# Planned margins behind transfers and GpSimd's mask, and the inverse's PSUM banks shared with value and z-gate projections

## Chip, cores and metric

The kernel runs on one core of a Trainium2 chip. The metric is the device time of one execution in microseconds, the median of the runs. One execution was also profiled; all durations and waits below come from that one.

## What is computed

The reference is a trunk of two layers over 2048 frames of width 1024, with a conditioning vector `c`. Layer 1 is a Griffin recurrent block, layer 2 a gated DeltaNet with 8 heads of 128:

```python
for i in range(DEPTH):                                   # DEPTH = 2
    cond = c_act @ ada_w[i] + ada_b[i]                   # shift, scale, gate
    h = rmsnorm(x, norm_g[i]) * (1.0 + scale) + shift
    if i % N_MIXERS == 0:
        out = rglru_block(h, ...)       # linear, conv4, RG-LRU scan, * silu(z), linear
    else:
        out = gated_deltanet_block(h, ...)
    x = x + gate * out
return rmsnorm(x, final_g)

# inside gated_deltanet_block, per head and chunk:
qkv = silu(causal_dwconv(proj[..., :o1], conv_w)); z = proj[..., o1:o2]
q = l2norm(q) * DK ** -0.5; k = l2norm(k)
t_mat = triangular_solve(a_mat + eye, eye)               # inverse of the chunk's matrix
v_new = u_c - w_c @ state
o_c = q_c @ state + attn_c @ v_new
state = state * e_c + k_c.T @ v_new                      # chunk after chunk
o = rmsnorm(o) * onorm_g * silu(z); out = o @ out_w
```

All of it is float32. Large products are made of three products of split operands (high x high, high x low, low x high).

## The kernel before

**Stages.** The frames are worked on in two units of 1024, each in two halves of 512 columns. Layer 1 comes first: its input projection (panels of 128 output columns, eight for the recurrent branch x and eight for its gate z), convolution, gates and scan, then its output projection. Layer 2 follows: for each unit and head the projections k, v, q and at some heads z (`KINDS`, `ZS`), then the heads' recurrences, and at the end the output projection with the final norm.

**One projection.** `job` (L667) takes a weight panel that `panels_thread` (L608) has loaded as `raw`, cast to `whi` on ScalarE (L640) and completed by `wlo` (GpSimd at L646 in the first unit, a reload in the second). It takes a PSUM bank, issues 24 matmuls of 128x512 (L664 in `products`), and hands the bank to a thread that empties it: `conv2_thread` (L984) for k, v and q, which copies it to `xe` on ScalarE (L726 in `extend`) and then convolves it on VectorE (L714), or `zgate_thread` (L1015) for z, which reads it on ScalarE (L1019) and again on VectorE (L1021).

**PSUM.** There are eight banks, two under each of four tags. In layer 2, `mm` holds all projections, `tp` transposes and the products k k and q k, `d` the recurrence's tiles, and `c` the tiles `px` and `pr` of the inverse (`levels_thread`, L1300 on) and `pab` of the decay. Buffers of one tag are used in turn, so a new tile waits until the last tile but one of its tag is given back.

**One head of layer 2.** `key_thread` (L1110) loads the decay rows `ec` by broadcast, masks them on GpSimd (L1119), takes the exponential on ScalarE (L1123), and forms the chunk's matrix `ac` (L1169), whose 32x32 blocks go to memory. `inverses_thread` inverts the blocks on VectorE (L1285 and L1288, 31 steps), `levels_thread` joins them with small matmuls. `norm_q_thread` (L1191) turns the query through memory and takes its squares on ScalarE (L1203, tile `junkq`). `value_thread` (L1227) turns the value through memory (`tokens_of`, L1213, into `vn`) and scales it on ScalarE (L1239). `recurrence_thread` runs the chunks one after the other: `pp` (L1405), `zt` on VectorE (L1414), `py` (L1422), `yt` on ScalarE (L1428), `pS` (L1434), and the state on VectorE (L1447). `outputs_thread` (L1474) scales the head's output by `ro` and writes it to memory.

**Activations of later units.** `turned_thread` (L514) with `turn_thread` (L497) and `scale_thread` (L442) normalizes blocks of 128 rows, transposes them through a memory tile `xt_d`, and reloads them as `xk`.

**What sets the order.** Every piece above is a generator. `Weave` (L66) is a planner: it holds a planned time when each engine, the queue of transfers and each buffer come free, always takes the thread that can start first (ties by a priority), and writes that thread's instructions. So the order of the planned starts is the order of the instructions in each engine's queue, and the engines then run their queues in order. All transfers go through the one queue of SyncE. A thread says with its `yield` what it uses:

```python
elif w[0] == "sp":
    self.free["sp"] = t + 0.48
    self.free["dma"] = max(t + 1.13, self.free["dma"]) + w[1] / 360e3
    th.t = self.free["dma"] + self.SEEN if len(w) < 3 or w[2] else t + 0.48
elif w[0] == "none":
    th.t = t + max(w[1], 0.0)
else:
    self.free[w[0]] = t + w[1]
    th.t = t + w[1] + (w[2] if len(w) > 2 else self.LAG[w[0]])
```

`yield "act", 0.95` means that ScalarE is taken for 0.95 us and that the thread goes on after that and a lag (0.2 us for GpSimd and TensorE, 0.3 us for the other two). A third number replaces the lag. `yield "none", x` lets the thread alone wait for x planned microseconds. None of these numbers is an instruction.

Of the kernel before, what the change touches and what calls it, by code (L numbers as in the profile page):

```python
# [30 lines left out]
TURN = 2  # L31
BLK = 2
KTN, QTN = 6, 5
EPS = 1e-6


# [102 lines left out]
def trunk_kernel(ctx, tc, x, c, ada_w, ada_b, ada_c, norm_c, final_g, w1, cw1, cb1, gate_w, gate_b, lam, ow1,  # L139
# [299 lines left out]
        w.set(ev("gates"))  # L439


    def scale_thread(xt, done):  # L442
        stok = yield slots["ss"]
        rtok = yield slots["rs"]
        ttok = yield slots["tt"]
        yield "act", 1.04
        junk = tile_([P, D], "tt", "sqj", BF16)
        ss = tile_([P, 1], "ss", "ss")
        act.activation(junk, xt, AF.Square, accum_out=ss)
        put("tt", ttok)  # L450
        yield "pool", 0.75
        rs = tile_([P, 1], "rs", "rs")
        rsqrt(rs, ss, 1.0 / D, 1)
        put("ss", stok)
        yield "dve", STT
        dve.tensor_scalar(xt, xt, rs, None, ALU.mult)
        put("rs", rtok)
        w.set(done)
# [36 lines left out]
            put(tag, tok)  # L495

    def turn_thread(key, t_d, xt, tok, ttok, b):  # L497
        yield from scale_thread(xt, ev("scaled", key, b))
        for d in range(2):
            htok = yield slots["hf"]  # L500
            yield "dve", EV
            tb = tile_([P, KT * 2, 32], "hf", "xb")
            dve.transpose(out=tb, in_=xt[:, d * TC:(d + 1) * TC].rearrange("p (a j) -> p a j", j=32))
            if d == 1:
                put("b4", tok)
            dst = t_d[4 * d:4 * d + 4, :, b * P:(b + 1) * P].rearrange("k (r i) (c j) -> c i (k r) j", i=32, j=32)
            for c_ in range(4):
                yield "sp", 64 * KB, c_ == 3
                sp.dma_start(out=dst[c_], in_=tb[32 * c_:32 * c_ + 32])
            put("hf", htok)  # L510
        put("turn", ttok)
        w.set(ev("turned", key, b))
# [95 lines left out]
    def panels_thread():  # L608
        yield ev("small")
        ahead = []  # L610
        for name, panels, _ in plans:
            for m, p in enumerate(panels):

                if m == 2 and name == ("in2", 0):
                    yield ev("owt", 1, 1)
                    yield ev("gates")
                if m == 0 and name == ("in1", 0):
                    for q in panels[0:2]:
                        ahead.append((yield from panel_load(name, q)))
                    w.set(ev("firstpanels"))  # L620
                if m in (2, len(panels) - 1) or m < 2 and name != ("in1", 0):
                    if name == ("in1", 0):
                        yield ev("adaissue", 3)
                    ahead.append((yield from panel_load(name, p)))
                htok = yield slots["whi"]
                ltok = yield slots["wlo"]
                if not ahead:
                    ahead.append((yield from panel_load(name, p)))
                raw, rtok = ahead.pop(0)
                lo = tile_([P, KT, P], "wlo", "wlo", F32R)  # L630
                if name[1] > 0:

                    kept = yield ev("kept", p)
                    yield "sp", 512 * KB, False
                    sp.dma_start(out=f(lo), in_=kept)
                    w.spawn(arrive_thread(ev("lo", name, p)), 0)
                yield ev("raw", name, p)
                yield "act", 0.95
                hi = tile_([P, KT, P], "whi", "whi", F32R)
                act.copy(hi, raw)  # L640
# [26 lines left out]
    def job(name, jobs, n):  # L667
# [6 lines left out]
        if layer == 2 and kind in "kq":  # L674
            rtok = yield slots[kind + "t"]

        bank = "d" if layer == 1 and kind == "z" else "mm"
        mtok = yield slots[bank]
        pt = ps.tile([P, TC], F32, tag=bank, name="mm")
        yield from products(pt, (hi, lo), h, (lambda k: ev("split", (name, i), k)), 0.2275 if layer == 1 else MM)  # L680
# [3 lines left out]
        if layer == 1:  # L684
            w.spawn((conv1_thread if kind == "x" else z1_thread)(u, m, i, pt, mtok, bank), 2, 0.2)
        elif kind == "z":
            w.spawn(zgate_thread(u, m, i, pt, mtok), 6, 0.2)
        else:
            w.spawn(conv2_thread(u, kind, m, i, pt, mtok, rtok), 5, 0.2)
        if all(j != i for _, j in jobs[n + 1:]):  # L690
            w.set(ev("free", name, i))
        w.set(ev("job", name, n))
# [23 lines left out]
    def extend(xe, pt, mtok, carry, key, g):  # L716

        if g == 0:
            yield "pool", 0.1
# [4 lines left out]
            pool.tensor_copy(out=xe[:, 0:4], in_=carry)  # L724
        yield "act", CP
        act.copy(xe[:, 4:4 + TC], pt)  # L726
        put("mm", mtok)
        yield "pool", 0.14, 0.0
        pool.tensor_copy(out=carry, in_=xe[:, TC:TC + 4])
        w.set(ev("carry", key, g))  # L730
# [250 lines left out]
        w.set(ev("l2"))  # L981


    def conv2_thread(u, kind, h, i, pt, mtok, rtok):  # L984
# [4 lines left out]
        yield from extend(xe, pt, mtok, carry2[:, idx, :], (kind, h), u * NTC + i)  # L989
        ftok = yield slots["xf"]  # L990
        yield "pool", 0.68
        xf = tile_([P, TC], "xf", "xf")
# [19 lines left out]
        put("tt", ttok)  # L1012
        w.set(ev(kind, u, h, i), (r, rtok))

    def zgate_thread(u, h, i, pt, mtok):  # L1015
# [5 lines left out]
        dve.scalar_tensor_tensor(tz, tz, 1.0, pt, ALU.add, ALU.mult)  # L1021
        put("mm", mtok)
# [87 lines left out]
    def key_thread(u, h, i):  # L1110
# [4 lines left out]
        yield "sp", 256 * KB  # L1115
        ec = tile_([P, TB, P], "ec", "ec")
        sp.dma_start(out=ec, in_=g_d[h:h + 1, i * TC:(i + 1) * TC].to_broadcast([P, TC]))
        yield "pool", 0.7
        pool.affine_select(out=ec, in_=ec, compare_op=ALU.is_ge, fill=-1e30, base=0, pattern=[[0, TB], [1, P]],  # L1119
                           channel_multiplier=-1)  # L1120
        for b in range(TB):
# [69 lines left out]
    def norm_q_thread(u, h, i):  # L1191
# [3 lines left out]
        yield "sp", 256 * KB  # L1195
        pq = tile_([P, TB, P], "hf", "pq")
        sp.dma_start(out=pq, in_=q_d.rearrange("b p d -> p b d"))
        stok = yield slots["ssq"]
        ss = tile_([P, TB], "ssq", "ssq")
        for b in range(TB):  # L1200
# [12 lines left out]
    def tokens_of(ap, name):  # L1213
# [7 lines left out]
        for r in range(4):  # L1221
            yield "sp", 64 * KB, r == 3
            sp.dma_start(out=dst[r], in_=tb[32 * r:32 * r + 32])  # L1223
        put("hf", htok)
        return t_d

    def value_thread(u, h, i):  # L1227
# [5 lines left out]
        yield "sp", 256 * KB  # L1233
        vn = tile_([P, TB, P], "vn", "vn")
        sp.dma_start(out=vn, in_=v_d.rearrange("b p d -> p b d"))
        nk, ntok = (yield ev("key", u, h, i))[-2:]
        for b in range(TB):
            yield "act", 0.255, 0.0
# [235 lines left out]
    def outputs_thread(u, h, i, oo, otok, so, sotok):  # L1474
# [1 line left out]
            yield ev("o", u, h, i * TB + b)  # L1476
        rq, qtok = yield ev("rq", u, h, i)
        rtok = yield slots["ro"]
        yield "pool", 1.4
        ro = tile_([P, TB], "ro", "ro")  # L1480
        rsqrt(ro, so, 1.0 / P, TB)
        pool.tensor_tensor(ro, ro, rq, ALU.mult)
# [16 lines left out]
        for g in range(4):  # L1499
            yield "sp", 128 * KB, g == 3  # L1500
            sp.dma_start(out=dst[g], in_=ob[32 * g:32 * g + 32])
        put("hf", htok)
        w.set(ev("od", u, h, i))

# [276 lines left out]
```

## Time and profile before

| what | value |
|---|---|
| median of 3 runs | 1968.5 us |
| the runs | 1966.23, 1968.5, 1977.2 us |
| the profiled execution | 1969.04 us |
| its span from first to last instruction | 1967.3 us |
| mean granted TensorE clock | 0.983 |
| TensorE busy | 1849.4 us (94%) |
| VectorE, ScalarE, GpSimd busy | 1469.3, 1050.9, 640.5 us |
| transfers | 322.77 MB |

PE is TensorE's matmuls, PEld its weight loads, DVE VectorE, ACT ScalarE, POOL GpSimd, SP SyncE, which issues the transfers. A row of waits reads "who <- what ended the wait: total us, times, longest us". A row of the timeline gives start and duration in us, engine, line, operation, written and read tiles, shapes and count, and in square brackets the idle time of the engine just before it with what ended it. The granted clock is a share of full speed; where it is 0.5 a matmul takes twice its time.

### The profile page before, as it was taken

To read this page: it belongs to the slowest core of one execution; us is meant where nothing else is said; L and a number is where in the kernel's file an instruction comes from. 1 tells how busy PE (TensorE), PEld (TensorE's weight loads), DVE (VectorE), ACT (ScalarE), POOL (GpSimd) and SP (SyncE) were. 2 spreads that over 40 slices of the span, in tenths; PEclk is the share of its full clock that TensorE was granted. 3 is DMA by queue.
4 is the path that set the end of the run, shared out by engine and by line. 5 is a ranking of instruction groups with operands and counts; after the bars stand their busy time and mean duration, and the time that the engine had idled before them with its cause. 6 is when DMAs were issued, how large, how long until landed. Compare 5 with 4: busy or idle time off the path is not lost.

```text
span 1967.3 us, 31401 instructions
## 1 busy us (share of the span) xinstructions
PE 1849.4 (94%) x10286; PEld 1501.0 (76%) x10286; DVE 1469.3 (75%) x3271; ACT 1050.9 (53%) x2585; POOL 640.5 (33%) x1116
## 2 busy tenths in 40 slices
PE   6999898999999999998889999998999999999998
PEld 3777677887777777786777777777888888878887
DVE  6898888887645577878787888667777778876653
ACT  3667577766121345564655666465566566654221
POOL 3354532223000235344434543232332334410101
PEclk8999999999999999999999999999999999999999
DMA  8476736555688334566774447365356455576751
GB/s 315 115 211 190 236 131 192 159 175 163 215 219 226 134 110 138 129 158 159 180 176 116 125 118 198 99 185 137 99 146 164 121 142 146 137 221 204 240 168 65
DMA packets 511724, 322.77 MB, mean 164 GB/s; under 512 B 371268, under 2 KB 439236, under 8 KB 511560
## 3 DMA queue, kind: packets, MB, share of 16 engines
q1 hardware_dynamic: 511560, 320.77, 57.8%
q8 instruction: 81, 1.33, 0.3%
q14 instruction: 83, 0.68, 0.1%
HBM read 219.93 MB, written 100.73 MB: 163 GB/s over the span
## 4 chain that ended last, share of the span: by engine, by line
PE 52%; DVE 17%; DMA 12%; ACT 6%; issue 6%; SPq 4%; POOL 3%; DVEq 0%; POOLq 0%; ACTq 0%
PE mm L664 28%; PE mmo L664 12%; DVE xf L714 3%; PE pg L803 2%; DMA raw<-in_w 2%; DVE tblk L1288 2%; DMA pq<-q_d 2%; DVE ttmp L1285 2%; SPq L1223 1%; DMA ada<-in_ada_w 1%; PE pkk L1165 1%; PE pS L1434 1%; ACT junkq L1203 1%; PE py L1422 1%; PE pp L1405 1%
## 5 line engine op out<-in xcount | busy, mean ns | idle before, releaser
L714 DVE SCALAR_TENSOR_TENSOR xf<-xe,cw_s,xf 128x512 f32<-128x512 f32 x288 | 237.6, 829 | 28.5 <-POOL xf L993 23.8
L646 POOL TENSOR_TENSOR wlo<-raw,whi 128x1024 fp32r<-128x1024 f32 x48 | 119.6, 2492 | 129.1 <-ACT whi L640 125.7
L640 ACT CAST whi<-raw 128x1024 fp32r<-128x1024 f32 x96 | 100.6, 1047 | 79.2 <-DMA raw<-in_w 55.0
L1285 DVE TENSOR_TENSOR ttmp<-blk,tblk 128x60 f32<-128x60 f32 (+24 forms) x496 | 114.4, 231 | 25.7 <-DMA blk<-blk_d 12.8
L1288 DVE TENSOR_TENSOR tblk<-tblk,ttmp 128x60 f32<-128x60 f32 (+24 forms) x496 | 123.6, 249 | 10.0 <-POOL tblk L1279 0.2
L664 PE MATMUL mm<-hh_('in2', 1)_12236,whi 128*128 128x512 f32 x256 | 105.7, 413 | 2.6 <-ACT xe L726 2.6
L664 PE MATMUL mm<-hh_('in2', 0)_5231,whi 128*128 128x512 f32 x256 | 104.8, 409 | 3.5 <-ACT xe L726 3.5
L664 PE MATMUL mm<-hh_('in2', 0)_5454,whi 128*128 128x512 f32 x256 | 104.3, 408 | 2.0 <-ACT xe L726 2.0
L664 PE MATMUL mm<-hl_('in2', 0)_5455,whi 128*128 128x512 f32 x256 | 105.2, 411 | 0.0
L664 PE MATMUL mmo<-oh,yl 128*128 128x512 f32 x256 | 101.7, 397 | 3.4 <-DVE yl L925 3.4
L664 PE MATMUL mm<-hh_('in2', 0)_5231,wlo 128*128 128x512 f32 x256 | 104.8, 409 | 0.0
L664 PE MATMUL mm<-hh_('in2', 1)_12236,wlo 128*128 128x512 f32 x256 | 104.6, 409 | 0.0
L664 PE MATMUL mm<-hl_('in2', 0)_5232,whi 128*128 128x512 f32 x256 | 104.5, 408 | 0.0
L664 PE MATMUL mm<-hh_('in2', 1)_12412,wlo 128*128 128x512 f32 x256 | 104.5, 408 | 0.0
L664 PE MATMUL mm<-hl_('in2', 1)_12237,whi 128*128 128x512 f32 x256 | 104.3, 407 | 0.0
L664 PE MATMUL mm<-hh_('in2', 0)_5454,wlo 128*128 128x512 f32 x256 | 104.1, 407 | 0.0
L664 PE MATMUL mmo<-oh,yh 128*128 128x512 f32 x256 | 101.3, 396 | 2.8 <-ACT yh L921 2.8
L664 PE MATMUL mm<-hl_('in2', 1)_12413,whi 128*128 128x512 f32 x256 | 103.2, 403 | 0.0
L664 PE MATMUL mm<-hh_('in2', 1)_12412,whi 128*128 128x512 f32 x256 | 103.1, 403 | 0.0
L664 PE MATMUL mmo<-oh,oh 128*128 128x512 f32 (+1 forms) x264 | 102.7, 389 | 0.2 <-DVE tz L1021 0.2
L664 PE MATMUL mmo<-ol,oh 128*128 128x512 f32 (+1 forms) x264 | 102.8, 390 | 0.0
L664 PE MATMUL mmo<-ol,yh 128*128 128x512 f32 x256 | 101.3, 396 | 1.4 <-DVE ol L905 1.4
(331 smaller groups left out, 5633.1 us busy)
## 6 DMA issues: line engine op xcount, KB each, us to landing
raw<-in_w SPq DMA_DIRECT2D x96, 512.0 KB, 4.2
araw<-in_ada_w SPq DMA_DIRECT2D x32, 512.0 KB, 4.5
xt<-x_d SPq DMA_DIRECT2D x32, 512.0 KB, 4.4
xt_d<-xb SPq DMA_DIRECT2D x192, 64.0 KB, 2.6
xk<-xt_d SPq DMA_DIRECT2D x24, 512.0 KB, 6.0
xt<-in_x SPq DMA_DIRECT2D x16, 512.0 KB, 5.1
ada<-in_ada_w SPq DMA_DIRECT2D x16, 512.0 KB, 7.7
y_d<-tz SPq DMA_DIRECT2D x32, 256.0 KB, 3.7
```

What stands on the lines that cost most here:

```text
L640: act.copy(hi, raw)
L646: pool.tensor_tensor(lo, raw, f(hi), ALU.subtract)
L664: pe.matmul(pt, lhsT=lhs[a][:, k, :], rhs=rhs[b][:, k, :], start=(k == 0 and n == 0), stop=(k == KT - 1 and n == 2))
L714: dve.scalar_tensor_tensor(xf, xe[:, 1 + j:1 + j + TC], wc[:, j:j + 1], xf, ALU.mult, ALU.add)
L803: pe.matmul(pg, lhsT=a[:, g, :], rhs=b, start=(q == 0), stop=(q == 2))
L1165: pe.matmul(pkk[:, b, :], lhsT=kc, rhs=kc, start=True, stop=True)
L1203: act.activation(junk, pq[:, b, :], AF.Square, accum_out=ss[:, b:b + 1])
L1223: sp.dma_start(out=dst[r], in_=tb[32 * r:32 * r + 32])
L1285: dve.tensor_tensor(tmp, blk[:, j, j + 1:32].unsqueeze(2).to_broadcast([P, r, c_]), t[:, j, 0:c_].unsqueeze(1).to_broadcast([P, r, c_]), A ...
L1288: dve.tensor_tensor(t[:, j + 1:32, 0:c_], t[:, j + 1:32, 0:c_], tmp, ALU.subtract)
L1405: pe.matmul(pp[:, 0, :], lhsT=kc, rhs=S_, start=True, stop=True)
L1422: pe.matmul(py, lhsT=rm[:, b, :], rhs=zt, start=True, stop=True)
```

## The change

It has two parts. First, a constant `MARGIN` of 2.4 planned microseconds is put, whole or half, behind some steps: behind the reloads of the query and the value (whole), behind the load of a weight panel in layer 2, before and behind GpSimd's mask, behind the rsqrt of the outputs and of the transposed activations, and behind the last of several stores before their `hf` buffer is given back (half). Second, in layer 2 the projections of kind v and z take a bank of tag `c` where they took one of `mm`; `extend` and `zgate_thread` get the tag as a parameter to give the right one back.

```diff
+MARGIN = 2.4
-    def scale_thread(xt, done):
+    def scale_thread(xt, done, late=False):
...
-        yield "pool", 0.75
+        yield "pool", 0.75, MARGIN / 2 if late else 0.2
         rs = tile_([P, 1], "rs", "rs")
...
     def turn_thread(key, t_d, xt, tok, ttok, b):
-        yield from scale_thread(xt, ev("scaled", key, b))
+        yield from scale_thread(xt, ev("scaled", key, b), True)
...
                 sp.dma_start(out=dst[c_], in_=tb[32 * c_:32 * c_ + 32])
+            yield "none", MARGIN / 2
             put("hf", htok)
...
                 yield ev("raw", name, p)
+                if name[0] == "in2":
+                    yield "none", MARGIN / 2
                 yield "act", 0.95
...
-        bank = "d" if layer == 1 and kind == "z" else "mm"
+        bank = ("d" if layer == 1 else "c") if kind in "vz" else "mm"
...
-            w.spawn(zgate_thread(u, m, i, pt, mtok), 6, 0.2)
+            w.spawn(zgate_thread(u, m, i, pt, mtok, bank), 6, 0.2)
-            w.spawn(conv2_thread(u, kind, m, i, pt, mtok, rtok), 5, 0.2)
+            w.spawn(conv2_thread(u, kind, m, i, pt, mtok, bank, rtok), 5, 0.2)
...
         act.copy(xe[:, 4:4 + TC], pt)
-        put("mm", mtok)
+        put(bank, mtok)
...
         sp.dma_start(out=ec, in_=g_d[h:h + 1, i * TC:(i + 1) * TC].to_broadcast([P, TC]))
-        yield "pool", 0.7
+        yield "none", MARGIN / 2
+        yield "pool", 0.7, MARGIN / 2
         pool.affine_select(out=ec, in_=ec, compare_op=ALU.is_ge, fill=-1e30, base=0, pattern=[[0, TB], [1, P]],
...
         sp.dma_start(out=pq, in_=q_d.rearrange("b p d -> p b d"))
+        yield "none", MARGIN
...
             sp.dma_start(out=dst[r], in_=tb[32 * r:32 * r + 32])
+        yield "none", MARGIN / 2
         put("hf", htok)
         return t_d
...
         sp.dma_start(out=vn, in_=v_d.rearrange("b p d -> p b d"))
+        yield "none", MARGIN
         nk, ntok = (yield ev("key", u, h, i))[-2:]
...
-        yield "pool", 1.4
+        yield "pool", 1.4, MARGIN / 2
         ro = tile_([P, TB], "ro", "ro")
...
             sp.dma_start(out=dst[g], in_=ob[32 * g:32 * g + 32])
+        yield "none", MARGIN / 2
         put("hf", htok)
         w.set(ev("od", u, h, i))
```

More of the change, by code (lines that the diff above doesn't have):

```diff
@@ L714, in taps, with extend @@
             dve.scalar_tensor_tensor(xf, xe[:, 1 + j:1 + j + TC], wc[:, j:j + 1], xf, ALU.mult, ALU.add)
-    def extend(xe, pt, mtok, carry, key, g):
+    def extend(xe, pt, mtok, bank, carry, key, g):
         if g == 0:
@@ L981, in phase1_end_thread, with conv2_thread @@
         w.set(ev("l2"))
-    def conv2_thread(u, kind, h, i, pt, mtok, rtok):
+    def conv2_thread(u, kind, h, i, pt, mtok, bank, rtok):
         yield ev("l2")
@@ L988, in conv2_thread @@
         xe = tile_([P, TC + 4], "xe", "xe")
-        yield from extend(xe, pt, mtok, carry2[:, idx, :], (kind, h), u * NTC + i)
+        yield from extend(xe, pt, mtok, bank, carry2[:, idx, :], (kind, h), u * NTC + i)
         ftok = yield slots["xf"]
@@ L1013, in conv2_thread, with zgate_thread @@
         w.set(ev(kind, u, h, i), (r, rtok))
-    def zgate_thread(u, h, i, pt, mtok):
+    def zgate_thread(u, h, i, pt, mtok, bank):
         ttok = yield slots["tt"]
@@ L1021, in zgate_thread @@
         dve.scalar_tensor_tensor(tz, tz, 1.0, pt, ALU.add, ALU.mult)
-        put("mm", mtok)
+        put(bank, mtok)
         yield "sp", 256 * KB
```

## Prediction

> **What bounds the kernel now.** I read the busy times first, then the busy times by stage, then the waits of TensorE in the stage that the change mostly touches, then the waits of ScalarE there, and last single moments of the timeline. First the page's head:
>
> ```profile
> span 1967.3 us, 31401 instructions
> PE 1849.4 (94%) x10286; PEld 1501.0 (76%) x10286; DVE 1469.3 (75%) x3271; ACT 1050.9 (53%) x2585; POOL 640.5 (33%) x1116
> ```
>
> TensorE works 94% of the span and nothing else comes near. So time is won only where TensorE stands still or runs at a lower clock. By stage (start, layer 1 with its output projection, layer 2's projections and recurrences, layer 2's output projection); the columns are the stretch, its length, the busy times of the engines with their instructions, the granted clock, and the DMA share and rate:
>
> ```profile
> 0.00:60.00 60.00, 40.27 (x143) 26.55 (x143) 41.94 (x87) 23.33 (x40) 21.11 (x36) 0.86 0.72 276
> 60.00:690.00 630.00, 602.59 (x2584) 480.89 (x2583) 472.88 (x692) 342.50 (x482) 185.42 (x182) 0.98 0.61 183
> 690.00:1760.00 1070.00, 1007.73 (x6545) 829.70 (x6544) 834.40 (x2330) 621.80 (x1918) 410.72 (x841) 0.99 0.56 145
> 1760.00:1960.00 200.00, 198.49 (x1020) 163.76 (x1019) 118.50 (x160) 62.00 (x143) 22.29 (x55) 1.00 0.57 177
> ```
>
> Layer 2's stage holds 1070.0 - 1007.7 = 62.3 us in which TensorE idles, and its clock of 0.99 loses some 10 us more. That is all the change can win there; the last stage has 1.5 us to give, and the start has none of the changed steps. What ends TensorE's waits in layer 2 (total, times, longest):
>
> ```profile
> PE pS L1434 <- ACT yt L1428: 12.3, 13, 1.7
> PE mm L664 <- ACT xe L726: 8.1, 5, 2.6
> PE pp L1405 <- DVE state L1447: 7.3, 6, 1.8
> PE pk L1130 <- DVE tblk L1288: 6.1, 3, 2.3
> PE py L1422 <- DVE zt L1414: 4.4, 5, 1.6
> ```
>
> Two rows are ScalarE's: the recurrence's small copy yt comes late, and the copy xe, which empties a projection's bank, comes late. The others are VectorE's lateness. Now what ScalarE itself stood waiting for in the same stage:
>
> ```profile
> ACT whi L640 <- DMA raw<-in_w: 30.9, 24, 3.0
> ACT junkq L1203 <- DMA pq<-q_d: 23.2, 20, 3.0
> ACT ec L1123 <- POOL ec L1119: 21.6, 17, 2.7
> ACT vn L1239 <- DMA vn<-v_d: 20.7, 13, 3.1
> ACT oo L1487 <- POOL ro L1482: 10.4, 10, 2.1
> ```
>
> These are 106.8 us in 84 waits, 1.3 us each, on work that no recurrence step needs at that moment, while whatever stands behind it in ScalarE's queue waits too, as here:
>
> ```profile
> 1374.31 0.31 ACT L1203 ACTIVATE junkq<-pq 128x128 bf16<-128x128 f32 x1 [1.90 <-DMA pq<-q_d]
> ...
> 1375.16 0.26 ACT L1428 ACTIVATE yt<-py 128x128 f32<-128x128 f32 x1
> ...
> 1375.48 0.49 PE L1434 MATMUL pS<-yt,kd 128*128 128x128 f32 x2 [0.86 <-ACT yt L1428]
> ```
>
> ScalarE stood 1.90 us for a query's transfer, the copy yt came behind it, and TensorE stood 0.86 us for yt.
>
> **Part 1, the banks.** No instruction is added or removed; the values' and z-gates' projections write to the two banks "c" instead of the two banks "mm". It removes the waits of a projection on a bank still full. Such a wait, and the clock after three of the five:
>
> ```profile
> 907.01 0.56 ACT L726 COPY xe<-mm 128x512 f32<-128x512 f32 x1
> ...
> 907.63 0.50 PE L664 MATMUL mm<-hh_('in2', 0)_5231,whi 128*128 128x512 f32 x1 [1.97 <-ACT xe L726]
> ```
>
> ```profile
> 727.00:731.00 4.00, 4.00 (x11) 3.17 (x12) 4.00 (x10) 1.45 (x5) 2.35 (x6) 0.57 0.42 136
> 907.50:911.50 4.00, 3.87 (x10) 3.09 (x11) 2.10 (x6) 2.36 (x5) 3.75 (x9) 0.57 0.68 168
> 1296.50:1300.50 4.00, 4.00 (x13) 3.19 (x13) 3.01 (x7) 1.53 (x2) 3.86 (x10) 0.58 0.71 177
> ```
>
> A clock of 0.57 over 4 us costs 0.43 x 4 = 1.7 us, three times 5.1 us. With the 8.1 us of waiting, 13.2 us hang on these banks. A query's or key's projection will find its bank last used by another query or key, with a value pair or a z pair in between, so I let all 13.2 go.
>
> The Trainium skill says otherwise of the clock: its page "TensorE: Matmul & The Clock Gate", section "HAM oscillation — how this bites in real kernels", asks only that TensorE not idle for more than about 3.4 us. By that rule waits of 2 us cost only themselves, and the sum below would end 5.1 us higher; the three rows, half speed right behind waits of at most 2.6 us, speak against it.
>
> What the banks cost is new waiting on "c". The trace has no such handover, so I bound it. Values and gates hold their bank long, and the inverse (px, pr) will meet them:
>
> ```profile
> 785.51 0.39 PE L664 MATMUL mm<-hh_('in2', 0)_5454,whi 128*128 128x512 f32 x1
> ...
> 805.76 0.69 DVE L1021 SCALAR_TENSOR_TENSOR tz<-tz,mm 128x512 f32<-128x512 f32 x1
> ```
>
> ```profile
> 1400.64 1.09 PE L1327 MATMUL px<-tf,ac 32*32 32x32 f32 x32
> ```
>
> ```profile
> 1407.26 0.59 ACT L726 COPY xe<-mm 128x512 f32<-128x512 f32 x1
> 1410.00 0.59 ACT L726 COPY xe<-mm 128x512 f32<-128x512 f32 x1
> ```
>
> The gate's bank is held from 785.51 to 806.45, 20.9 us. At 1400.64, with both values of that head not yet copied out, the inverse would have to wait for the copy that ends at 1407.85, 7.2 us later. Since the order is planned, such a delay mostly becomes another place for px in TensorE's queue, filled with projections, and costs nothing as long as filler is there. What costs is a handover later than planned. Lower end: 0. Upper end: as many late ones among the 128 new tiles on "c" (64 of the inverse, 64 values and gates) as there were among the 128 on "mm", 13.2 us. I take a third, 4.4 us, because px and pr are small tiles that are read out soon, unlike a projection's. Banks: -13.2 + 4.4 = -8.8 us (from -13.2 to 0).
>
> **Part 2, the margins.** They are waits of the planner alone: no instruction, no semaphore. They place the dependent instruction later in its engine's queue: 2.4 us for the query's squares and the value's scaling, 1.2 us for a weight's cast, 1.2 us before and 1.0 us more behind GpSimd's mask, 1.0 us more behind ro, and 1.2 us before an hf buffer is passed on. The waits they aim at are 1.3 us in the mean and 3.1 us at most, so most of the 106.8 us of ScalarE's standing should go. TensorE gains only what it stood behind these: at most the 12.3 us for yt, at least 0. The rows that name ScalarE's stalls are many and the example shows the link, but yt also has its own latency behind py; I take half, -6 us.
>
> What stands later and is covered: the squares, the values, the mask and the output scale come up to 2.4 us later in each head; TensorE has projections to run meanwhile. Without that cover a head would pay up to 2.4 us, 16 x 2.4 = 38 us. The casts wait 1.2 us more behind their transfer, in front of a panel that lasts two projections of 24 matmuls, over 10 us at 0.23 us each. In the transposed loads each block of 128 rows takes 1.0 + 2 x 1.2 = 3.4 us longer; eight blocks go two at a time, at most 13.6 us. Here is the last piece of the first half of the loaded activations against its first use, in layer 1 and in layer 2:
>
> ```profile
> 228.75 0.82 ACT L559 ACTIVATE h<-xk,cond 128x512 f32<-128x512 f32 x1 [2.04 <-POOL hl_('in1', 1)_1903 L570]
> ```
>
> ```profile
> 265.86 0.40 PE L664 MATMUL mm<-hh_('in1', 1)_1902,whi 128*128 128x512 f32 x1
> ```
>
> ```profile
> 645.90 0.82 ACT L559 ACTIVATE h<-xk,cond 128x512 f32<-128x512 f32 x1 [0.71 <-POOL hl_('in2', 0)_5232 L570]
> ```
>
> ```profile
> 673.22 0.39 PE L664 MATMUL mm<-hh_('in2', 0)_5231,whi 128*128 128x512 f32 x1
> ```
>
> There are 36 and 26 us to spare, so I cost these at nothing. At the end, the last head's output is written, read back, gated, and used from the output projection's ninth block on:
>
> ```profile
> 1826.27 1.94 SPq L1501 DMA_DIRECT2D o_d<-ob  x4
> ...
> 1830.08 0.34 SPq L1548 DMA_DIRECT2D on<-o_d  x1
> ```
>
> ```profile
> 1846.40 1.05 ACT L1567 CAST oh<-zs 128x1024 fp32r<-128x1024 f32 x1 [0.35 <-DVE zs L1557]
> ```
>
> ```profile
> 1769.00:1870.90 101.90, 94.49 (x385) 70.28 (x386) 20.75 (x30) 1.00 0.74 226
> ```
>
> The last row counts the output projection's matmuls: at 48 a block, 384 end the eighth block at about 1870.9. The load at 1830 is ready by some 1850, so about 20 us are spare against 7.2 us of a late inverse and 3.4 us of margins.
>
> **The sum.** The profiled execution took 1969.0 us (span 1967.3 and 1.7 around it), 0.5 us over the median of the runs. 1969.0 - 8.8 - 6.0 = 1954.2 us; I forecast 1954.
>
> **The rivals.**
>
> VectorE takes over. TensorE's waits named on VectorE (7.3 + 6.1 + 4.4 = 17.8 us in the rows above alone) are untouched, and its 834.4 us of work in 1070 leave little air. If the next thing that TensorE stands for is VectorE wherever ScalarE now comes in time, the margins win nothing, and the banks only their net: 1969.0 - 8.8 = 1960.2; with half the banks' gain lost as well, 1964.6. For it: VectorE's rows are the most numerous. Against: the five bank waits end in a ScalarE copy. 19%.
>
> The margins do not do what they say. The planner moves the load as well as its user, for the same queue serves all transfers, and a transfer put behind others lands as late as before. The time is again 1960.2. Against: the waits are short next to the margin. 8%. The Trainium skill's rule on the clock, 1954.2 + 5.1 = 1959.3, would land beside these two and is counted with them.
>
> The handovers on "c" are late, and it gets slower. TensorE works in order: px in its queue, waiting for a bank whose copy is late, holds all projections behind it. One late handover costs 8.1 / 5 = 1.6 us, and 1.7 us of clock in three of five, together 2.6 us. The gains of 13.2 + 6.0 are eaten by 7.4 late ones among 128; at 11 of them, fewer than one in a head, 28.6 - 19.2 = +9.4 us, 1978. For it: gates held for 20.9 us, and px tied to the recurrence. Against: only 5 in 128 were late before, with the same copies. 15%.
>
> **How the numbers follow.** What a measurement can tell from no change is about 0.5%, 9.8 us. My forecast of a gain above that has 58% and its own range of 1938 to 1959: the low end is all of 13.2 and 12.3 with some 5 us more of VectorE's waits that begin behind ScalarE. The two rivals near 1960 to 1965 make up 27% for no change, the last one 15% for slower. To leave out no more than a fifth the range goes from 1938 to 1977.
>
> **What would show it.** Right: the row of mm waiting for xe gone or under 2 us, no half clock at those three places, ScalarE's waits for pq, vn, raw and ec below half of their 96.4 us, yt's row near 6 us, layer 2's idle near 50 us. Wrong on the banks: new rows of px, pr or mm waiting for xe, tz or tf of more than 5 us. Wrong on the margins: ScalarE's waits gone and yt's row still at 12 us, or these waits unchanged. A gap before 265 or 673 us, or in the output projection's second half, would refute the cover that I named.

## The result and the profile after

The changed kernel takes 1944.3 us in the median (1942.2 to 1950.5, four runs) beside 1967.6 us before (the three runs above and a fourth). The recorded ratio of the two kernels is 0.9868, with a 95% interval of 0.9845 to 0.9892. I had forecast 1954 us: the sign was right, and 9.7 us of the gain were missing in my sum. The head of the changed kernel's page:

```profile
span 1940.5 us, 31373 instructions
PE 1846.8 (95%) x10286; PEld 1505.6 (78%) x10286; DVE 1479.8 (76%) x3271; ACT 1045.5 (54%) x2587; POOL 647.4 (33%) x1116
```

TensorE does the same work. The span is 26.8 us shorter, and TensorE's idle time fell from 117.9 us (1967.3 - 1849.4) to 93.7 us: nearly the whole gain is TensorE standing less. Where, is seen in the busy times by stage, cut at the first matmul of each stage: layer 1's input projection, its output projection, layer 2 up to its last recurrence, layer 2's output projection. The columns are as in the prediction. Before:

```profile
36.40:479.50 443.10, 418.73 (x1800) 336.71 (x1799) 375.28 (x575) 299.85 (x431) 165.71 (x154) 0.97 0.56 174
479.50:673.20 193.70, 185.20 (x783) 146.91 (x782) 111.03 (x152) 47.98 (x62) 22.28 (x30) 0.99 0.75 217
673.20:1769.70 1096.50, 1033.22 (x6689) 848.62 (x6687) 847.18 (x2356) 632.28 (x1936) 415.59 (x851) 0.99 0.56 144
1769.70:1967.30 197.60, 190.14 (x950) 157.05 (x950) 113.11 (x149) 57.37 (x135) 21.60 (x55) 0.99 0.55 170
```

After:

```profile
36.20:474.80 438.60, 418.50 (x1808) 336.75 (x1807) 382.36 (x582) 294.59 (x428) 167.75 (x152) 0.98 0.58 179
474.80:667.20 192.40, 183.85 (x776) 147.56 (x776) 102.94 (x138) 50.80 (x63) 22.50 (x30) 0.97 0.72 208
667.20:1739.60 1072.40, 1028.88 (x6640) 849.81 (x6639) 856.96 (x2350) 625.51 (x1931) 421.05 (x851) 0.99 0.57 147
1739.60:1940.50 200.90, 193.38 (x1001) 159.93 (x999) 116.00 (x162) 61.20 (x146) 21.45 (x58) 0.99 0.55 169
```

Layer 2 gained 24.1 us and the last stage lost 3.3 us, but the cut falls a little earlier in the work after the change: some 50 matmuls moved from the one to the other (6689 to 6640, 950 to 1001). The two together are 20.8 us shorter, and TensorE's idle time in them fell by 19.8 us, all of it in layer 2 (63.3 to 43.5 us). Layer 1's input projection gained 4.5 us, about as much as two executions of one and the same order differ there (see below). What ends TensorE's waits in layer 2 now (690 to 1760 us; total, times, longest):

```profile
PE pp L1413 <- DVE state L1455: 5.6, 8, 1.7
PE pqk L1258 <- DVE qt L1014: 5.3, 4, 3.0
...
PE pS L1442 <- ACT yt L1436: 2.6, 5, 1.0
PE pr L1347 <- DVE tz L1025: 2.4, 1, 2.4
...
PE px L1335 <- DVE tz L1025: 2.1, 1, 2.1
...
PE mm L668 <- ACT xe L730: 0.8, 1, 0.8
```

Both of ScalarE's rows are nearly gone: yt from 12.3 to 2.6 us (3.6 us with a second, new row for it), xe from 8.1 to 0.8 us. What stays is VectorE's. Added up over the whole of layer 2's stage as cut above, TensorE's waits that ScalarE ends fell from 24.2 to 4.8 us, and those that VectorE ends stayed where they were, 37.6 and 37.7 us. ScalarE's own standing in the stage:

```profile
ACT whi L644 <- DMA raw<-in_w: 22.0, 11, 5.8
ACT ec L1128 <- POOL ec L1124: 6.9, 4, 3.3
...
ACT oo L1495 <- POOL ro L1490: 5.3, 3, 2.4
ACT junkq L1209 <- DMA pq<-q_d: 4.6, 5, 1.4
...
ACT vn L1247 <- DMA vn<-v_d: 0.2, 1, 0.2
```

The five rows were 106.8 us and are 39.0 us. So ScalarE's standing fell as the prediction said, and the reward for TensorE is larger.

### The profile page after: what moved, and what is told of

Its sections match the earlier page's. It is cut to its first block, busy times and chain, and to the rows that moved or that the text cites. A ratio compares the mean times of both kernels' runs of the same rounds, so it can differ in the third digit from the quotient of the medians.

```text
span 1940.5 us, 31373 instructions
## 1 busy us (share of the span) xinstructions
PE 1846.8 (95%) x10286; PEld 1505.6 (78%) x10286; DVE 1479.8 (76%) x3271; ACT 1045.5 (54%) x2587; POOL 647.4 (33%) x1116
## 4 chain that ended last, share of the span: by engine, by line
PE 51%; DVE 22%; DMA 10%; ACT 6%; issue 4%; SPq 4%; POOL 2%; DVEq 0%; POOLq 0%; ACTq 0%
PE mm L668 25%; PE mmo L668 15%; DVE xf L718 4%; DVE ttmp L1293 2%; DVE tblk L1296 2%; PE pg L807 2%; DMA blk<-blk_d 1%; DMA raw<-in_w 1%; DMA ada<-in_ada_w 1%; DVE xf L756 1%; PE pp L1413 1%; PE pS L1442 1%; PE py L1430 1%; PE pS L1443 1%; ACT junk L1146 1%
## 5 line engine op out<-in xcount | busy, mean ns | idle before, releaser
L668 PE MATMUL mm<-hh_('in2', 0)_5342,whi 128*128 128x512 f32 x256 | 105.6, 413 | 0.8 <-ACT xe L730 0.8
L668 PE MATMUL mm<-hh_('in2', 0)_5437,wlo 128*128 128x512 f32 x256 | 105.3, 411 | 0.0
L668 PE MATMUL mm<-hh_('in2', 1)_12057,whi 128*128 128x512 f32 x256 | 104.9, 410 | 0.0
L668 PE MATMUL mm<-hl_('in2', 0)_5438,whi 128*128 128x512 f32 x256 | 104.9, 410 | 0.0
L668 PE MATMUL mm<-hh_('in2', 0)_5437,whi 128*128 128x512 f32 x256 | 104.7, 409 | 0.0
L668 PE MATMUL mm<-hh_('in2', 1)_12057,wlo 128*128 128x512 f32 x256 | 104.5, 408 | 0.0
L668 PE MATMUL mm<-hl_('in2', 0)_5343,whi 128*128 128x512 f32 x256 | 104.1, 407 | 0.0
L668 PE MATMUL mm<-hl_('in2', 1)_12307,whi 128*128 128x512 f32 x256 | 103.9, 406 | 0.0
L668 PE MATMUL mm<-hh_('in2', 0)_5342,wlo 128*128 128x512 f32 x256 | 103.7, 405 | 0.0
L668 PE MATMUL mm<-hh_('in2', 1)_12306,wlo 128*128 128x512 f32 x256 | 103.5, 404 | 0.0
```

Source lines behind the costliest of these rows:

```text
L668: pe.matmul(pt, lhsT=lhs[a][:, k, :], rhs=rhs[b][:, k, :], start=(k == 0 and n == 0), stop=(k == KT - 1 and n == 2))
```

## The experiments

Each stands against the kernel before, run again beside it; its median there was 1970.7, 1971.7 or 1971.1 us, and the ratios go by that.

### The two parts apart

The banks alone: the changed kernel with

```diff
-MARGIN = 2.4
+MARGIN = 0.0
```

and the old lags of 0.2 us behind GpSimd's steps.

> The banks of the change without its margins (all margins at nothing). Theory A (each part removes its own stall): TensorE's waits for the copy xe fall from 8.1 us to under 2 us, its waits for yt stay near 12 us, ScalarE's waits for pq, vn, ec and raw in layer 2 stay near 96 us; time 1967.6 - 9 = 1958 us (1955 to 1962), layer 1 unchanged to within 2 us. Theory B (any new plan moves the time by chance, the parts do not matter): anything from 1945 to 1975, with no relation to these rows. Theory C (the margins carry it all): 1967 us.

Measured: 1973.0 us, ratio 1.0014 (0.9994 to 1.0035). No gain of the banks alone can be seen. TensorE's waits in layer 2 of that kernel:

```profile
PE pqk L1258 <- DVE qt L1014: 13.3, 7, 3.9
PE pS L1442 <- ACT yt L1436: 12.7, 13, 2.1
...
PE px L1335 <- DVE tz L1025: 2.6, 1, 2.6
...
PE pr L1347 <- DVE tz L1025: 1.8, 1, 1.8
```

The row for xe is gone, as I had said, and the late handovers to the inverse cost only 2.6 + 1.8 = 4.4 us. That this is the very figure that I had set is luck: my third of 13.2 us had no measurement behind it. Still nothing is won. The row of qt was this before:

```profile
PE pqk L1250 <- DVE qt L1010: 2.5, 2, 2.0
```

It grew by 10.8 us. Over the whole stage TensorE's waits that ScalarE ends fell by 11.5 us (24.2 to 12.7), and those that VectorE ends rose by 10.7 us (37.6 to 48.3). I read this as TensorE arriving earlier at something that VectorE has not finished; the totals fit it, but no run shows it wait by wait. ScalarE's own waits for pq, vn, raw and ec, which I had expected to stay near 96 us, rose to 117.9 us.

The margins alone:

```diff
-        bank = ("d" if layer == 1 else "c") if kind in "vz" else "mm"
+        bank = "d" if layer == 1 and kind == "z" else "mm"
```

> The margins of the change with the old banks. Theory A: waits for xe stay near 8 us, waits for yt fall to near 3 us, layer 1 about 6 us shorter as in the changed kernel; time about 1967.6 - 16 = 1952 us (1948 to 1957). Theory B: anything from 1945 to 1975. Theory C: 1944 us.

Measured: 1948.9 us, ratio 0.9885 (0.9858 to 0.9911). The interval overlaps with that of the whole change, so the margins alone bring a gain that cannot be told from the whole one, and no gain of the banks on top of them is shown. Layer 2's stage and TensorE's waits in it:

```profile
672.60:1749.60 1077.00, 1026.62 (x6690) 851.44 (x6688) 858.87 (x2362) 630.50 (x1940) 424.61 (x851) 0.99 0.57 146
```

```profile
PE pk L1135 <- DVE kt L1014: 9.4, 4, 4.6
...
PE mm L668 <- ACT xe L730: 3.9, 4, 1.9
```

No row for yt is left, and xe's has halved without any change of banks: about half of the waiting that I had credited to the banks goes with the margins alone. The stage is 19.5 us shorter (1096.5 to 1077.0), of which 12.9 us are idle time (63.3 to 50.4). The other 6.6 us lie in TensorE's busy time at practically the same number of matmuls; no row says which of them got shorter. The last stage was 4.4 us longer in this execution (202.0 us). The expected 6 us in layer 1 did not show: its input projection took 443.4 us, with the same order as in the changed kernel.

### Is it the margins, or any new order?

A planner gives another order for any number that is touched. So one duration was moved, with no reason behind it:

```diff
-    STT, EV, CP, TR, MM, M4 = 0.665, 0.605, 0.48, 0.109, 0.2163, 0.218
+    STT, EV, CP, TR, MM, M4 = 0.665, 0.605, 0.48, 0.109, 0.2163, 0.222
```

> The kernel before with one number of the planner changed from 0.218 to 0.222 us (the planned time of a small matmul): a new plan of layer 2 with no margin and the old banks. Theory A: within 5 us of 1967.6 us, waits for yt and xe together still over 15 us. Theory B: as far from 1967.6 us as the changed kernel is, 10 us or more either way.

Measured: 1966.2 us, ratio 0.9977 (0.9962 to 0.9992). One arbitrary re-plan moves the time by some 4.5 us. The margins' 22 us are about five times that. What follows has to be read with this yardstick: a part worth 4 us or less cannot be told from a chance of the order. One re-plan is a small sample; what speaks for the margins as well is that the five kernels that hold those at the mask and behind ro at 2.4 us, with VectorE's planned times as they were, lie at 0.9851 to 0.9916.

The yardstick holds for rows of waits too. I had expected yt and xe together above 15 us; they were at 12.5 us, because this re-plan took most of xe's row away without touching a bank:

```profile
PE mm L664 <- ACT xe L726: 2.0, 1, 2.0
```

So the missing row in the run of the banks does not prove by itself what the banks did. Nor does a wait that is gone show in the time at once: here layer 2 idled 52.6 us in place of 63.3, but TensorE was busy 6.1 us longer with as many matmuls, at a clock of 0.98 for 0.99.

Single stages have a yardstick of their own. In six kernels (the one before, the banks alone, this one, and below the reloads, the mask with ro, the mask alone) the four engines run layer 1 in the same order. Yet its input projection took between 443.1 and 446.6 us, and layer 2 began between 671.3 and 677.3 us. The changed kernel and the margins alone share another order there and took 438.6 and 443.4 us. So some 5 us in layer 1, read from one profile each, say little.

### Which margin

Five kernels, each the one before with some of the margins, and one that leaves some out. The margins of layer 2's turned loads were not run alone. The reloads of query and value:

```diff
         sp.dma_start(out=pq, in_=q_d.rearrange("b p d -> p b d"))
+        yield "none", MARGIN
...
         sp.dma_start(out=vn, in_=v_d.rearrange("b p d -> p b d"))
+        yield "none", MARGIN
```

> The kernel before with only the margins behind the reloads of the query and the value (old banks). Theory A (TensorE gains what it stood behind ScalarE's stalls, in proportion to them; the margins together gave 22 us): ScalarE's stalls for pq and vn, 43.9 us of 106.8 before, fall under 8 us, the others stay; TensorE's waits for yt fall from 13 us to about 6 us; 1968 - 9 = 1959 us. Theory D (the gain comes from the plan as a whole being looser, not from one stall): less than 5 us, 1965 us, with the stalls gone all the same.

Measured: 1960.6 us, 0.9950 (0.9933 to 0.9967). ScalarE's waits in layer 2:

```profile
ACT whi L641 <- DMA raw<-in_w: 47.6, 30, 3.7
...
ACT ec L1124 <- POOL ec L1120: 27.7, 16, 4.5
...
ACT junkq L1205 <- DMA pq<-q_d: 3.2, 3, 1.4
```

TensorE's:

```profile
PE mm L665 <- ACT xe L727: 12.0, 6, 5.4
...
PE pS L1437 <- ACT yt L1431: 3.6, 6, 1.1
```

The query's wait fell from 23.2 to 3.2 us and the value's row is gone, while the mask's rose from 21.6 to 27.7 us and the weights' from 30.9 to 47.6 us: contrary to what I had expected, the others did not stay. TensorE's wait for yt fell from 12.3 to 3.6 us, but the one for xe rose to 12.0. I take it that the next ScalarE copy behind a stall pays.

Around the mask and behind ro:

```diff
-        yield "pool", 0.7
+        yield "none", MARGIN / 2
+        yield "pool", 0.7, MARGIN / 2
...
-        yield "pool", 1.4
+        yield "pool", 1.4, MARGIN / 2
```

> The kernel before with only the margins at GpSimd's mask and behind ro (old banks). Theory A: ScalarE's stalls for ec and oo, 32.0 us before, fall under 12 us, the others stay; 1968 - 7 = 1961 us. Theory D: less than 5 us, 1965 us.

Measured: 1952.6 us, 0.9906 (0.9888 to 0.9925), the largest part. ScalarE's waits:

```profile
ACT junkq L1205 <- DMA pq<-q_d: 26.1, 15, 5.2
...
ACT oo L1489 <- POOL ro L1484: 6.9, 5, 2.2
...
ACT ec L1125 <- POOL ec L1121: 0.5, 1, 0.5
```

Here the mask's row went and the query's stayed. The gain of 18.5 us is more than twice what Theory A allowed, although the weights' row rose to 47.4 us here too and ScalarE's five rows together still make 90.9 of 106.8 us. So the gain does not follow the sum of these rows; what else the two margins did is open. Next the mask's two lines without the one at ro:

> The kernel before with only the margins around GpSimd's mask (old banks, no margin at ro). Mask and ro together gave 18 us, twice what ScalarE's waits for ec and oo had TensorE lose. Theory F (the mask is worth more because it also blocks GpSimd's queue, in which the convolution's first product and the rsqrts stand behind it): nearly all of it is the mask's, 1970 - 17 = 1953 us, ScalarE's waits for ec near 1 us, VectorE's waits for GpSimd (xf, cc) clearly below the kernel before. Theory D (any loosening of the plan gains): about half, 1961 us.

Measured: 1962.9 us, 0.9959 (0.9939 to 0.9980). That is less than half of the 18.5 us, although the mask's row on ScalarE is as good as gone here too:

```profile
ACT oo L1489 <- POOL ro L1484: 14.6, 13, 2.8
...
ACT ec L1125 <- POOL ec L1121: 1.1, 3, 0.6
```

So the idea fell that the mask's place in GpSimd's queue explains the whole part. GpSimd's other customers fare no better for it: VectorE's wait for the decay product cc was 11.3 us before and is 25.1 us here.

```profile
DVE ec L1159 <- POOL cc L1156: 25.1, 15, 6.5
```

The rest, some 10 us, would then belong to the single margin at ro, whose users wait 14.6 us here and 6.9 us with it. That is a difference between two kernels, two of the yardstick above; the margin at ro was not timed alone.

The casts of layer 2's weights and the `hf` buffers of query, value and output:

```diff
+                if name[0] == "in2":
+                    yield "none", MARGIN / 2
...
             sp.dma_start(out=dst[r], in_=tb[32 * r:32 * r + 32])
+        yield "none", MARGIN / 2
         put("hf", htok)
```

> The kernel before with only the margins behind layer 2's weight loads and before the hf buffers of queries, values and outputs are passed on (old banks). Theory A: ScalarE's stalls for raw, 30.9 us before, fall to about 20 us as in the changed kernel; VectorE's waits for stores get shorter; 1968 - 4 = 1964 us. Theory D: the same number, so this run weighs little between them; a gain over 8 us would speak for D.

Measured: 1968.8 us, 0.9998 (0.9982 to 1.0014). A zero made of two parts:

```profile
36.50:488.10 451.60, 423.55 (x1806) 339.42 (x1805) 380.55 (x581) 300.70 (x433) 167.77 (x154) 0.96 0.55 173
...
683.80:1764.50 1080.70, 1034.15 (x6690) 851.93 (x6688) 849.23 (x2355) 629.12 (x1934) 416.95 (x848) 0.99 0.57 146
```

Layer 2 gained 15.8 us (1096.5 to 1080.7), and layer 1's input projection lost 8.5 us (443.1 to 451.6), 5 us against the slowest of the kernels with the old order of layer 1. The time shows neither.

The turned loads of layer 1, where `scale_thread` is late and the `hf` buffer held only for `in1`:

```diff
-        yield from scale_thread(xt, ev("scaled", key, b))
+        yield from scale_thread(xt, ev("scaled", key, b), key[0][0] == "in1")
...
+            if key[0][0] == "in1":
+                yield "none", MARGIN / 2
             put("hf", htok)
```

> The kernel before with only the margins in layer 1's transposed loads; layer 2 keeps its order of before. Theory A1 (these margins shorten layer 1): 1968 - 5 = 1963 us, layer 1's projection near 439 us against 443 us. Theory B1 (the difference between the two profiles in layer 1 is that of two executions): 1968 us within 2 us.

Measured: 1968.1 us, 0.9979 (0.9963 to 0.9995); and the opposite, the whole change with these margins kept for `in2` only:

> The changed kernel without the margins in layer 1's transposed loads (the squares' rsqrt and the stores before their hf buffer is passed on); layer 2 keeps all of its own. Layer 1 then has the order of before. Theory A1 (layer 1's 6 us come from these margins): layer 1 ends 6 us later than in the changed kernel, 1950 us in all. Theory B1 (nothing in layer 1 stalls on them): 1944 us, layer 1 no longer than in the changed kernel.

Measured: 1955.8 us, 0.9916 (0.9889 to 0.9942). Layer 1's input projection lasts 438.0 us in the first and 451.4 us in the second, beside 443.1 before and 438.6 in the whole change. By the profiles these margins are worth 5 us alone and 13 us once the weights' margin is there: with it and without them the stage is at 451.6 and 451.4 us, and with both at 438.6, or at 443.4 in the margins alone. The timings say 4 us alone, the size of the arbitrary re-plan, and 0.5% in the whole, where the two intervals just touch. One thing goes with these margins at 2.4 us in the nine profiles that I compared: the last store of layer 1's turned activations starts at 196.1 to 196.7 us in the three kernels with them (this one, the margins alone, the whole change), and at 204.1 to 206.9 us in six without. So with them the turning ends 7 to 11 us earlier; how was not followed.

Summed up, the parts give about 10 + 18.5 + 0.4 + 4 = 33 us, and all margins together 22 us. The difference of 11 us is little more than the intervals allow (3 to 4 us either way for each part, 5 us for the whole). That the parts do not add up is likely, then, and would fit that behind each stall in ScalarE's queue stands the same next wait, VectorE's; no run tests this.

### Is a longer margin better?

```diff
-MARGIN = 2.4
+MARGIN = 4.8
```

> The changed kernel with margins twice as long (4.8 instead of 2.4). ScalarE's waits were 1.3 us in the mean and 3.1 us at most, so they are covered already. Theory A: the stalls that are left fall further, at most 3 us are won and some 3 us lost on later buffers: 1944 us within 5 us. Theory D (looser is better): 1935 us or less. Theory B (a new plan, a new chance): 10 us or more either way.

Measured: 1982.5 us, ratio 1.0063 (1.0042 to 1.0084), slower than before. What is covered at 2.4 is not at 4.8. The reload of the second unit's activations in this kernel, and after it in the changed kernel:

```profile
1248.06 14.11 SPq L546 DMA_DIRECT2D xk<-xt_d  x5
```

```profile
1181.23 1.61 SPq L546 DMA_DIRECT2D xk<-xt_d  x2
```

The reload starts 67 us later, and the second unit's projections have no input until then. It starts right behind the last store of the turned activations that it reads. All 64 stores, in the changed kernel and in the doubled one (the shortest, median and longest issue in ns, then the start of the first and of the last in us):

```profile
L510 SPq DMA_DIRECT2D xt_d<-xb x64: 303/492/2935, 881.3 to 1088.1; - x64
```

```profile
L510 SPq DMA_DIRECT2D xt_d<-xb x64: 303/490/1914, 886.7 to 1247.0; - x64
```

In the kernel before they went from 882.5 to 1017.1 us. So the turning, 134.6 us long before, takes 206.8 us at 2.4 and 360.3 us at 4.8; the time left between its end and the reload goes from 175 to 93 to 1 us. The doubled kernel over 38 us around the reload:

```profile
1229.00:1267.00 38.00, 27.83 (x119) 21.52 (x117) 12.53 (x35) 15.65 (x45) 3.92 (x6) 0.51 0.53 142
```

Of these 119 matmuls only 5 are a projection's. With little but the recurrences left, TensorE is busy 27.8 of 38 us, 73%, at half the clock. The first unit's part of layer 2 lasts 593.6 us in place of 550.1. These 43.5 us are more than the 38 us by which this kernel is slower than the changed one.

### Would a truer plan for VectorE help?

If VectorE ends most waits now, its planned times might be too short. They were raised to what the trace shows, 0.8 us where the plan had 0.665 in this row of the changed kernel's groups (layer 2, 690 to 1740 us; count, then busy us and mean ns, then the idle time before them):

```profile
L718 DVE SCALAR_TENSOR_TENSOR xf<-xe,cw_s,xf 128x512 f32<-128x512 f32 x282 | 225.5, 803 | 15.9 <-POOL xf L997 12.0 <-ACT yt L1436 1.3
```

The edit, on top of the whole change:

```diff
-    STT, EV, CP, TR, MM, M4 = 0.665, 0.605, 0.48, 0.109, 0.2163, 0.218
+    STT, EV, CP, TR, MM, M4 = 0.8, 0.69, 0.48, 0.109, 0.2163, 0.218
...
-            dur = 0.065 + r * c_ / 960.0
+            dur = 0.18 + r * c_ / 960.0
```

> The changed kernel with the planner's times for VectorE put up to what the profile shows (convolution step 0.80 for 0.665 us, whole-tile steps 0.69 for 0.605 us, each step of the block inverse 0.115 us more). What TensorE still waits for in layer 2 is nearly all VectorE's, 37.7 of 42.5 us. Theory G (it is late because the plan takes it for faster than it is): TensorE's waits for VectorE in layer 2 fall from 38 to about 20 us, time 1944 - 15 = 1929 us. Rival (VectorE's lateness is load, not plan): no gain or a loss, 1944 us or more.

Measured: 2054.3 us, ratio 1.0427 (1.0411 to 1.0442). The theory fell. Layer 2's stage, and what ends TensorE's waits in the recurrence (over the whole execution):

```profile
675.10:1827.00 1151.90, 1070.60 (x6564) 880.61 (x6563) 817.04 (x2272) 624.82 (x1899) 415.35 (x845) 0.93 0.53 136
```

```profile
PE py L1430 <- DVE zt L1422: 18.5, 31, 1.7
PE pp L1413 <- DVE state L1455: 14.2, 30, 0.9
PE pS L1442 <- ACT yt L1436: 11.2, 31, 0.4
```

The waits did not go, they multiplied: 31 for zt in place of 4 in the changed kernel, with a clock of 0.93 where it was 0.99. In the stage TensorE's waits for VectorE came to 57.6 us, where the theory had about 20. TensorE now meets a small latency at many steps of the recurrence, 0.4 to 0.6 us each in the mean. Why the plan with the short VectorE times interleaves better was not followed further.

### The seam between the layers

In the changed kernel TensorE stands before the first output products of layer 1, between 470 and 520 us, for the split weights oh and ol of that projection; one of the copies oh on ScalarE itself stood 5.0 us for the transfer of its weights:

```profile
PE mmo L668 <- ACT oh L907: 5.0, 2, 3.9
...
PE mmo L668 <- DVE ol L909: 3.0, 2, 2.2
```

So the weights' margin was left out for the first two panels:

```diff
-                if name[0] == "in2":
+                if name == ("in2", 1) or name[0] == "in2" and m > 1:
```

> The changed kernel without the margin behind the loads of layer 2's first two weight panels, which come while layer 1 goes over into its output projection; these loads share the raw buffers with that projection's weights. In every profile so far with the weight margin TensorE waits 5.8 to 8.0 us at 490 to 504 us for the split weights oh and ol at a clock of 0.90, in those without it 1.1 to 3.9 us at 0.93 to 1.00. Theory E (this margin delays the output projection's weights by keeping a raw buffer planned as taken): waits there fall to 4 us or less, layer 1 ends 5 to 8 us earlier, time 1944 - 6 = 1938 us. Rival (the waits come from the new order of layer 1's transposed loads): no change, 1944 us.

Measured: 1941.4 us, ratio 0.9851 (0.9835 to 0.9867). The same rows of that kernel:

```profile
PE mmo L668 <- DVE ol L909: 2.7, 2, 1.9
PE mmo L668 <- ACT oh L907: 1.2, 1, 1.2
```

The waits went from 8.0 to 3.9 us, as expected, and layer 1 with its output projection from 631.0 to 625.8 us, little more than two executions of one order differ (631.0 and 635.3 us in the changed kernel and in the margins alone). Only some 3 us of the time followed in place of 6, and the interval overlaps with the change's. It is the lowest of all ratios, but not shown to beat the change.

## Why the prediction was right, and where it was not

**What bounds the kernel.** Right. TensorE's busy time stayed (1849.4 and 1846.8 us), and 24.2 of the 26.8 us are idle time that it lost. I had said that layer 2 would keep an idle of some 50 us; by the stage's own limits it kept 43.5 of 63.3 us.

**The banks: the term that failed on its net.** "Banks: -13.2 + 4.4 = -8.8 us (from -13.2 to 0)." Measured alone: +2.3 us by medians, an interval that holds zero. Both halves of the term were seen as drawn: the row for xe went, and the new handovers took 4.4 us. What the step left out is what TensorE meets 2 us earlier, and the clock behind the new handovers (next paragraph). The totals of that run, 11.5 us less behind ScalarE and 10.7 us more behind VectorE, are those of the rival "VectorE takes over", to which I gave 19%, for this part. The range's end at 0 lies in the measured interval.

**The clock.** My test, the three places in time, was a poor one, since everything stands at other times after the change. Told by what stands before them: layer 2 held seven pieces of 3.41 us at half clock before, three of them behind waits for xe; it holds seven such pieces and one of 6.83 us after, none of them behind xe. So it loses as much to the clock as before, 11.9 us before and 15.4 us after. The 5.1 us that I counted were not won: most of the pieces now stand behind waits that VectorE ends. Two stand right behind the handovers on "c" that the change made, the waits of 2.4 and 2.1 us for tz in the rows above. The second, a wait that ended at 1176.42 us, is followed by this stretch:

```profile
1176.80:1183.60 6.80, 6.80 (x87) 5.83 (x85) 1.57 (x5) 5.28 (x17) 3.04 (x6) 0.50 1.04 267
```

These two pieces, 3.41 and 6.83 us, cost 5.1 us of clock. With their 4.5 us of waiting the handovers took 9.6 us in the changed kernel, where I had set 4.4 us for waiting and clock together; in the banks alone no such piece stood behind them. The rule of the Trainium skill that I had weighed against the rows (page "TensorE: Matmul & The Clock Gate", section "HAM oscillation — how this bites in real kernels", an idle of more than about 3.4 us) is not borne out by the doubled margin either: there the clock stood at 0.51 for 38 us, while the waits in that stretch, of which 1.7 us was the longest, looked like this:

```profile
PE py L1430 <- DVE zt L1422: 2.7, 6, 0.4
...
PE py L1430 <- DVE ac L1377: 1.7, 1, 1.7
```

**The margins: the term that was too small.** "TensorE gains only what it stood behind these: at most the 12.3 us for yt, at least 0." I took half, 6 us; alone they gave 22 us. The mechanism was right for the margins as a whole: 106.8 us of ScalarE's standing became 39.0 us (34.4 us with the margins alone), yt's row 2.6 us where I had said near 6, and of the 19.8 us of idle time that layer 2 lost, 19.4 us are waits that ScalarE had ended. Part by part the link is loose: the mask with ro won 18.5 us while ScalarE's five rows fell only to 90.9 us, and the reloads won 10 us with 87.4 us left. The upper end was drawn around one tile. Everything behind the stall in ScalarE's queue was late, xe and the inverse's tf as well, so at least all 24.2 us that ScalarE ends belonged into the bound. And VectorE waits for ScalarE and GpSimd too: its waits that these two end fell in layer 2 from 134.7 to 93.2 us. That its earlier steps shorten TensorE's waits is argued here, not shown; the waits of TensorE that VectorE ends stayed at 37.7 us.

**The covers.** At 2.4 they held. No wait for a late activation appeared at the two starts that I had shown, and the second half of the output projection idles 7.0 us before and after. At 4.8 one fell: the load of layer 2's second unit, the one of the three turned loads for which I had shown no row. My cost for such a load, "at most 13.6 us", was wrong as well: its stores took 72 us longer at 2.4 (134.6 to 206.8 us). What saved it was a slack of 175 us that the prediction does not show, not the smallness of the cost. Why the turning stretches by so much more than its margins was not followed.

"I cost these at nothing" was wrong for the turned loads of layer 1 too, with the sign of a gain: 4 us alone, no more than an arbitrary re-plan moves, and some 9 us in the whole change (0.9916 against 0.9868, whose intervals just touch). One cost I had not named: with the margin of the casts and without that of layer 1's turned loads, layer 1's input projection took 451.6 and 451.4 us in two kernels, 5 us more than the slowest with the old order. By the end of layer 1 it is less clear: layer 2 began at 683.8 us in the one and at 677.2 us in the other, the latter within the spread of the old order.

**The rivals.** "The margins do not do what they say" fell with the 39.0 us. "The handovers on c are late" showed its mechanism at 4.4 us, far from the 28.6 us that it needed. That the sum was near the truth is partly luck, a cancellation: 8.8 us or more too much for the banks, some 16 us too little for the margins.

## What to carry to other kernels

In an in-order queue a stall costs whoever stands behind it, so bound it by all waits that end in that engine, not by the one tile of the example. A wait that is taken away is worth at most the distance to the next one; the banks, which gave nothing, fit this. A margin about as long as the waits that it is to hide served here (2.4 us against 1.3 in the mean and 3.1 at most); twice that uncovered a transfer and cost more than the whole gain. No other lengths were run. And a re-plan needs its own yardstick, for the time and for each stage, before a few microseconds of it are explained.

## What the runs showed of the hardware

The clock fell to half not only behind a wait of 2 us, but for as long as TensorE's work stayed thin: 38 us at 0.51 with single waits of at most 1.7 us. TensorE was busy 73% of that time, but with stretched matmuls: those of 128x512 took 0.58 to 0.77 us there, where the whole kernel before has means near 0.41 us.

Many gaps of some tenths of a microsecond can cost as much by the clock as by themselves. In the kernel with truer VectorE times layer 2's stage ran at 0.93 in place of 0.99. Against the changed kernel its idle time rose by 37.8 us (43.5 to 81.3), and TensorE's busy time by 41.7 us (1028.9 to 1070.6) with 76 matmuls fewer.
